# Order of the last scan group, spaced blocks for three weight tiles, and one changed row order in a hybrid decoder step

## The chip, the cores and the metric

The kernel is one launch on 1 core of one Trainium2 chip. The metric is the device time of a launch in microseconds (us). The version before was timed in 3 runs: median 1778.77 us, from 1777.38 to 1779.85.

## The reference, cut to what matters

One layer of a hybrid decoder is computed for 336 tokens (16 meta tokens, 256 prompt tokens, 8 sequences of 8 sample tokens), model width 2048, in float32:

```
h = rms_norm(x);  proj = h @ w_in          # z | x,B,C | dt | sc_b | sc_c | sc_h | sc_z | g_a | g_b
xbc = silu(causal_dwconv(x,B,C));  y, state = ssd_chunked(...)       # 64 heads in 8 groups
y   = gated_group_rms_norm(y + d_skip * xs, z);   y_a = y @ w_ssd_out
u   = sc_c * sc_h;  y_b = (sc_b * causal_dwconv(u) * silu(sc_z)) @ w_sconv_out
out = x + (sigmoid(g_a) * y_a + sigmoid(g_b) * y_b) @ w_o ;  final rms_norm
```

The gated norm divides each of the 8 groups (512 columns) of `y * silu(z)` by the root of its own mean square, so a group's output block `y @ w_ssd_out` needs that group's whole scan first.

## The kernel before, in words

**Products.** Every activation and every weight block is split into a high and a low part of the type that TensorE multiplies at full rate (`hi` by a copy on ScalarE, L101; `lo` by a subtraction on VectorE, L102), and each product is three matmuls: high by high, high by low, low by high. Weights come in blocks of 128x1024 through the SyncE queue (L98) into `wraw`, `whi` and `wlo`, three buffers each. A `unit` (two blocks, 48 matmuls, one PSUM buffer `pj` of two) gives 128 output columns for all tokens; the order of its 16 rows of weights is a plan: `SEVEN` starts at row 6 and steps by -2, `FIVE` likewise with another turn, a plain number starts at that row. In `whi` and `wlo` a 128-column block sits every 144 elements (`WS`, 576 bytes), and a start offset (`AT_O` and others, in 16 elements) is chosen for the activation that it meets. Three weight tiles are not stored so: `wd` (the 64 time-step columns, `tables`, L349 on) and `eh`, `el` (the last two output blocks, L833), whose blocks stand one behind the other, 512 bytes apart.

**Stages.** First the short convolution branch (pool `pa`): u's 16 columns are made by `conv_in`, the second of them (`j == 1`) straight from the unnormalised input split. Then `tables` makes the time steps and decays of all heads. Then the scan (pool `pb`), one group `g` of 8 at a time. Last, the output projection (pool `pc`): 14 blocks as units, the last two through `eh` and `el`, once with `hx` moving (L885) and once with `hx` as the weights (`tokens`, L911).

**One scan group.** `ssd(g)` is a generator with 24 stops. `weave` (L795 on) runs main units and lets the generator take its steps between them, `NSTEP` = 23 steps spread evenly over the units' weights (a unit of 48 matmuls weighs 2, an output block of 24 weighs 1). The main units of a group are `z_units` (4 units, the gate of the norm), `out_units(g-1)` (8 blocks that multiply the previous group's normalised output `yh`, `yl` and add into `ya`, L767), and `conv_units(g+1)` (6 units). Groups 0 and 7 have `gate_units` too (the g_a columns; each unit is a tanh on ScalarE and a store). In group 7 there are no conv units; before the change its order is z, out(6), gate 4 to 7. After the group come `out_units(7)` and `gate_units(8..15)`. Steps of the generator that matter here:

- step 13 sums the scan's output in PSUM and adds the parts to `ys`; steps 14 and 15 gate it with z and square it; step 16 adds the squares on GpSimd (L713) and loads the sample states' operands
- step 17 splits the sum of squares into `zq` (ScalarE L716, VectorE L717). `zq` has the one buffer of `yh`:

```
zq = pb.tile([P, 4, T], F32R, name="zq", tag="yh", bufs=1)[:, :, :TV]
...
yh = pb.tile([P, 4, T], F32R, name="yh", bufs=1)[:, :, :TV]
yl = pb.tile([P, 4, T], F32R, name="yl", bufs=1)[:, :, :TV]
```

- step 18 sums over the partitions with two matmuls (L721, PSUM buffer `ms`), takes a reciprocal root on ScalarE (L723, a function table of its own is loaded for it) and refines it twice on VectorE (six operations, L726 to L728)
- step 19 updates the prompt state (L608, `ms`) and the first half of the sample states (L736, `yb`; L739 on VectorE), step 21 scales `ys` and splits it into the new `yh`, `yl` (L749, L750, L751), step 22 is the second half of the sample states.

**What sets the order.** A tile framework plans each engine's queue ahead of the launch: it goes by the order of the program, lets an instruction pass another when the first must wait, and hands a buffer of a tag on only when every instruction that uses its last holder is done, wherever that instruction stands in the program. Matmuls into the same PSUM tag keep their order. `behind` adds that a step's instructions stand behind the last main unit's on each engine.

Of the kernel before, what the change touches and what calls it, by code (L numbers as in the profile page):

```python
# [8 lines left out]
F32R = mybir.dt.float32r  # L9
AF = mybir.ActivationFunctionType  # L10
# [3 lines left out]
P = 128  # L14
T = 336
WS, WB = 144, 1280
META = 16
TC = 12
TV = T - META
DM = 2048  # L20
KT = DM // P
NB = 8
NG = 8
NH = 64
# [3 lines left out]
NA, NBT = 192, 128  # L28
UE = 2
# [11 lines left out]
def fb(ap):  # L41
    return ap.bitcast(F32)
# [7 lines left out]
def tile_hybrid_step(ctx, tc, xT, w0, w1, w2, wdt, wso, wsc, wo, cmask, vec, hvec, convst, sconvst, xe_, fwe, h0T,  # L50
                     yA, yB, yE, convo, ssmp, ssms, sconvo):
    nc = tc.nc
    mult, add, sub = ALU.mult, ALU.add, ALU.subtract
# [19 lines left out]
    hx = keep.tile([P, 2, KT, T], F32R, name="hx")  # L73
    hhi, hlo = hx[:, 0], hx[:, 1]
# [16 lines left out]
    AT_V, AT_Y, AT_O, AT_X, AT_U = 1, 3, 3, 1, 2  # L91
# [20 lines left out]
                                                                         mybir.DependencyReason.DATA), reason="step")  # L112

    row = [0]
    SEVEN, FIVE, ON = (6, (7, 5, 5, 5), -2), (6, (5, 5, 5, 5), -2), (None, (5, 5, 5, 5), -2)

    def terms(plan, half, hi, lo, xh, xl, nk):
# [52 lines left out]
    def eights(ap, w=8):  # L170
        return ap.rearrange("p (b t) -> p b t", t=w)
# [17 lines left out]
    with tc.tile_pool(name="pa", bufs=2) as pa:  # L189
# [4 lines left out]
        raw = []  # L194
# [28 lines left out]
        for k in range(KT):  # L223
# [5 lines left out]
            if k % 2 == 0 or k == 1:  # L229
                o = slice(384 * k, 384 * k + 384) if k < 2 else slice(0, 768)  # L230
# [4 lines left out]
            for i, t0 in enumerate((TC, TC, META)):  # L235
                o = 384 * (k % 2) + i * P
                for j, (w, x) in enumerate(((hi, uhi), (hi, ulo), (lo, uhi))):
                    nc.tensor.matmul(pu[i][:, :T - t0], w[:, o:o + P], x[:, k, t0:],  # L238
                                     start=k == 0 and j == 0, stop=k == 15 and j == 2)
# [4 lines left out]
        def conv_in(j, pr, pre=None, fac=None, between=None, at=0):  # L244
            c_s = pa.tile([P, T - TC], F32, name="c_s")
            if fac is None:
                nc.scalar.activation(c_s, pre[0] if pre else pr(w2[16 + j], TC, SEVEN, at), AF.Copy)
            else:
                nc.vector.tensor_tensor(c_s, pr(w2[16 + j], TC, SEVEN, at), fac, mult)
            if between:  # L250
                between()
            ph = pre[1] if pre else pr(w2[32 + j], TC, ON, at)
            up = pa.tile([P, 338], F32, name=f"up{j}" if j < 2 else "up", bufs=1 if j < 2 else 2)
            ups = eights(up[:, 258:338], 10)
            nc.vector.tensor_tensor(up[:, :258], c_s[:, 2:260], ph[:, 2:260], mult)  # L255
            nc.vector.tensor_tensor(ups[:, :, 2:10], eights(c_s[:, 260:]), eights(ph[:, 260:]), mult)
            return up, ups
# [73 lines left out]
        for j in range(KT):  # L331
            u = ((up0, ups0), (up1, ups1), u2)[j] if j < 3 else conv_in(j, proj)
# [6 lines left out]
            if 4 < j < 7:  # L339
                o = j - 5  # L340
# [7 lines left out]
        def tables(pt):  # L348
            raw = wp.tile([P, 1024], F32, name="wraw")  # L349
            nc.sync.dma_start(raw, wdt)  # L350
            wd = pt.tile([P, KT, 2, NH], F32R, name="wd", bufs=1)
            nc.scalar.activation(wd[:, :, 0, :], eights(raw, NH), AF.Copy)
            nc.vector.tensor_tensor(wd[:, :, 1, :], eights(raw, NH), fb(wd[:, :, 0, :]), sub)
            pd = ps.tile([P, 512], F32, name="pj")
            for k in range(KT):
                w = wd[:, k].rearrange("p i h -> p (i h)")
                nc.tensor.matmul(pd[:, :T], w, hhi[:, k, :], start=k == 0, stop=False)
                nc.tensor.matmul(pd[:, :T], w, hlo[:, k, :], start=False, stop=k == KT - 1)
            yield
            xl = pt.tile([NH, T], F32, name="acc", bufs=1)  # L360
            nc.scalar.activation(xl, pd[NH:, :T], AF.Copy)
# [105 lines left out]
    with tc.tile_pool(name="pb", bufs=2) as pb:  # L467
# [51 lines left out]
        def z_units(g, st):  # L519
            st["zs"] = []  # L520
            for t in range(4):
                pz = proj(w1[4 * g + t], META, (0, 3, 3, 3, 1, 3, 2, 0)[g])
                z = pb.tile([P, TV + 4], F32, name="zs", bufs=4)
                th = pb.tile([P, 360], F32, name="cth", bufs=1)[:, :TV]
                nc.scalar.activation(th, pz, AF.Tanh, scale=0.5)
                nc.scalar.activation(z[:, :TV], pz, AF.Copy)
                nc.vector.scalar_tensor_tensor(z[:, :TV], th, 1.0, z[:, :TV], add, mult)
                st["zs"].append(z)
                yield
# [240 lines left out]
        def gate_units(m0, m1):  # L770
            for m in range(m0, m1):
                pg = proj(w2[64 + m], META, 2 if m in (6, 7) else 0)
                if m < KT // 2:
                    th = pb.tile([P, 360], F32, name="cacc")[:, :TV]
                else:
                    th = pb.tile([P, TV + 4], F32, name="zs", bufs=4)[:, :TV]
                nc.scalar.activation(th, pg, AF.Tanh, scale=0.5)
                if m < KT // 2:
                    nc.sync.dma_start(sg_d[m], th)
                else:  # L780
                    old = pb.tile([P, 360], F32, name="cacc")[:, :TV]
                    nc.sync.dma_start(old, sg_d[m - KT // 2])
                    pair = [(q, t, fetch(q)) for q, t in ((m, th), (m - KT // 2, old))]
                    with tc.issue_after(latest["dve"]):
                        for q in pair:
                            merge(*q)
                yield
# [25 lines left out]
            pass  # L813
        for g in range(NG):
            parts = [(z_units(g, S[g]), 4, 2)]
            if g:
                parts.append((out_units(g - 1, S[g - 1]), 8, 1))
            if g in (0, NG - 1):
                parts.append((gate_units(0, 4) if g == 0 else gate_units(4, 8), 4, 2))
            if g < NG - 1:  # L820
                parts.append((conv_units(g + 1, S[g + 1]), 6, 2))
            weave(parts, ssd(g, S[g]))
# [5 lines left out]
    with tc.tile_pool(name="pc", bufs=3) as pc_:  # L828
# [1 line left out]
            nc.scalar.activation(hhi[:, m, :TV], ya[:, m, :TV], AF.Copy)  # L830
            nc.vector.tensor_tensor(hlo[:, m, :TV], ya[:, m, :TV], fb(hhi[:, m, :TV]), sub)
        KE, W, PT = KT - UE, NA // 2, UE * P
        eh, el = (pc_.tile([P, UE, 2 * 1024], F32R, name=n, bufs=1) for n in ("eh", "el"))  # L833
        sacc = pc_.tile([P, TV], F32, name="sacc", bufs=1)
        fA = pc_.tile([P, KT, NA], F32, name="fA", bufs=1)
        fB = pc_.tile([P, KE, NBT], F32, name="fB", bufs=1)
# [34 lines left out]
        for m in range(KE, KT):  # L871
            xr = pc_.tile([P, TV], F32, name="xr")[:, :NA]
            nc.sync.dma_start(xr, xk[:, m, META:META + NA])
            po = ps.tile([P, 512], F32, name="pj")
            for half in range(2):
                o = 1024 * half
                raw = wp.tile([P, 1024], F32, name="wraw")
                nc.sync.dma_start(raw, wo[m][:, o:o + 1024])
                h, l = eh[:, m - KE, o:o + 1024], el[:, m - KE, o:o + 1024]
                nc.scalar.activation(h, raw, AF.Copy)  # L880
                nc.vector.tensor_tensor(l, raw, fb(h), sub)
                for wide in ((True, False), (False, True))[half]:
                    for k in range(8):
                        w, x = (h, hx[:, :, 8 * half + k, :NA]) if wide else (l, hhi[:, 8 * half + k, :NA])
                        nc.tensor.matmul(po[:, :(1 + wide) * NA], w[:, k * P:k * P + P], x,  # L885
                                         start=half + k == 0 and wide, stop=half == 1 and k == 7 and wide)
                if m == KT - 1 and half == 0:
                    with tc.issue_after(nc.cur_bb.bb.instructions[-1]):
                        p0 = ps.tile([P, 512], F32, name="ms")
                        for i in range(2):  # L890
                            column(p0, i, sacc, i * W, W)
                        column(p0, 2, sacc, NA, NBT)
                        for q, w in ((slice(0, 2), W), (slice(2, 3), P)):
                            nc.vector.tensor_scalar(sm[:w, q], p0[:w, q], 1.0 / DM, EPS, mult, add)
                        nc.vector.tensor_scalar(r[:, 3:4], p0[:, 2:3], 1.0, EPS * DM, mult, add)
                        nc.gpsimd.tensor_tensor(yt[:, PT:], r[:, 3:4], up_, ALU.pow)
            nc.vector.scalar_tensor_tensor(xr, po[:, :NA], 0.5, xr, mult, add)
            nc.vector.scalar_tensor_tensor(ya[:, m, :NA], po[:, NA:2 * NA], 0.5, xr, mult, add)
            s_ = pc_.tile([P, TV], F32, name="sqf")[:, :NA]
            nc.scalar.activation(s_, ya[:, m, :NA], AF.Square)  # L900
            if m < KT - 1:
                nc.gpsimd.tensor_tensor(sacc[:, :NA], sacc[:, :NA], s_, add)
            nc.scalar.activation(ya[:, m, :NA], ya[:, m, :NA], AF.Copy, scale=col(V_FW, m))
# [3 lines left out]
        def tokens(a, b):  # L907
            for k in range(a, b):
                x = hx[:, :, k, NA:TV]
                for j, (h, w) in enumerate(((0, eh), (1, eh), (0, el))):  # L910
                    nc.tensor.matmul(pt_, x[:, h, :], w[:, :, k * P:k * P + P], start=k == 0 and j == 0,  # L911
                                     stop=k == KT - 1 and j == 2)
            return nc.cur_bb.bb.instructions[-1]

# [144 lines left out]
```

## Time and profile before

| | |
|---|---|
| median of 3 runs | 1778.77 us |
| the profiled execution, whole | 1779.76 us |
| its span from first to last instruction | 1777.9 us |
| TensorE matmuls, busy | 13006, 1768.5 us |
| VectorE busy | 1145.9 us |
| ScalarE busy | 828.6 us |
| mean granted TensorE clock | 0.999 |

All rows are of one profiled execution. TensorE is busy in nearly all of the span, so a saving has to come from its matmuls following each other more closely or from its few waits; busy time of the other engines counts only where TensorE waits for them. A matmul's own duration is longer than the distance to the next one, since they overlap: what a matmul costs is the distance from start to start.

### The profile page before, as it was taken

What the parts mean: (1) busy time and instruction counts of PE and PEld (TensorE: products, weight loads), DVE (VectorE), ACT (ScalarE), POOL (GpSimd) and SP (SyncE); (2) the same over time, 40 slices, a digit from 0 to 9 for tenths busy, and PEclk for the clock granted to TensorE, in tenths of its full rate; (3) what the DMA queues carried; (4) which work ended last, traced back from release to release, by engine and by line L of the source; (5) the groups of instructions that cost most, each with busy time, mean ns of one, the idle gap of its engine ahead of it and who ended that gap; (6) DMA issues with size and microseconds to landing.
All of it is one profiled execution on the core that took longest, in us unless ns stands there. A gap on an engine that the chain in (4) does not pass through costs nothing.

```text
span 1777.9 us, 32410 instructions
## 1 busy us (share of the span) xinstructions
PE 1768.5 (99%) x13006; PEld 1751.2 (98%) x13006; DVE 1145.9 (64%) x1696; ACT 828.6 (47%) x1269; POOL 392.9 (22%) x398
## 2 busy tenths in 40 slices
PE   9999999999999999999999999999999999999998
PEld 9999999999999999999999999999999999999998
DVE  7845544544643335668587787877878778776644
ACT  6433333333333334645656454564546556343543
POOL 0100000000000001253253433434334252400012
PEclk9999999999999999999999999999999999999999
DMA  7444444444444557467466574665756657577553
GB/s 258 152 155 153 156 153 155 151 155 155 157 162 159 169 166 237 151 187 248 160 211 222 184 247 155 213 218 183 249 158 215 211 176 254 156 247 220 190 182 128
DMA packets 117286, 331.33 MB, mean 186 GB/s; under 512 B 20944, under 2 KB 37904, under 8 KB 117136
## 3 DMA queue, kind: packets, MB, share of 16 engines
q1 hardware_dynamic: 116272, 327.89, 56.9%
q8 instruction: 102, 1.67, 0.4%
q10 hardware_dynamic: 864, 1.38, 0.2%
q14 instruction: 48, 0.39, 0.1%
HBM read 296.34 MB, written 32.88 MB: 185 GB/s over the span
## 4 chain that ended last, share of the span: by engine, by line
PE 88%; DVE 5%; DMA 4%; ACT 2%; issue 1%; POOLq 0%; SPq 0%; POOL 0%; ACTq 0%; DVEq 0%
PE pj L133 81%; DMA wraw<-w 3%; PE yb L673 2%; DVE wlo L102 1%; DMA ssms<-h 1%; DVE h L739 1%; PE ms L659 1%; PE pj L238 1%; ACT whi L101 1%; DVE cacc L494 1%; ACT W L582 1%; PE yb L608 1%; PE pj L885 1%; PE ms L238 0%; PE yb L911 0%
## 5 line engine op out<-in xcount | busy, mean ns | idle before, releaser
L133 PE MATMUL pj<-hx,whi 128*128 128x320 f32 (+2 forms) x5760 | 894.7, 308 | 0.0
L133 PEld LDWEIGHTS pj<-hx,whi 128*128 128x128 f32 x5760 | 846.9, 188 | 4.7 <-ACT pad L485 1.7
L102 DVE TENSOR_TENSOR wlo<-wraw,whi 128x1024 fp32r<-128x1024 f32 x470 | 597.6, 1272 | 384.6 <-ACT whi L101 200.7
L101 ACT ACTIVATE whi<-wraw 128x1024 fp32r<-128x1024 f32 x470 | 496.5, 1057 | 719.3 <-PE pj L133 589.4
L133 PE MATMUL pj<-hx,wlo 128*128 128x320 f32 (+2 forms) x2880 | 473.5, 307 | 0.0
L133 PEld LDWEIGHTS pj<-hx,wlo 128*128 128x128 f32 x2880 | 430.7, 188 | 0.0
L619 POOL TENSOR_TENSOR h<-h,decS 128x512 f32<-128x512 f32 x64 | 76.4, 1227 | 141.8 <-PE ms L659 141.8
L133 PE MATMUL pj<-yh,whi 128*128 128x320 f32 x512 | 95.3, 308 | 2.6 <-DVE yan L767 1.4
L261 POOL COPY SCS<-up 128x2 f32<-128x2 f32 x16 | 20.9, 1303 | 346.1 <-DVE up L255 315.9
L133 PE MATMUL pj<-yl,whi 128*128 128x320 f32 x512 | 93.6, 305 | 0.0
L133 PE MATMUL pj<-yh,wlo 128*128 128x320 f32 x512 | 93.4, 304 | 0.0
L494 DVE SCALAR_TENSOR_TENSOR cacc<-pad,V,cacc 128x360 f32<-128x360 f32 (+1 forms) x144 | 89.7, 623 | 2.0
L767 DVE TENSOR_TENSOR yan<-yan,pj 128x320 f32<-128x320 f32 x112 | 53.8, 484 | 55.8 <-PE pj L133 55.5
L133 PEld LDWEIGHTS pj<-yh,whi 128*128 128x128 f32 x512 | 78.9, 188 | 5.9 <-DVE yan L767 2.2
L487 POOL COPY pad<-cs 128x24 f32<-128x24 f32 x48 | 56.2, 1172 | 126.4 <-DVE cacc L494 117.7
L133 PEld LDWEIGHTS pj<-yl,whi 128*128 128x128 f32 x512 | 78.7, 188 | 0.0
L133 PEld LDWEIGHTS pj<-yh,wlo 128*128 128x128 f32 x512 | 78.5, 188 | 0.0
L488 POOL COPY cs<-pad 128x3 f32<-128x3 f32 x48 | 45.4, 946 | 79.0 <-ACT pad L485 78.5
L867 POOL TENSOR_TENSOR sacc<-sacc,sqf 128x320 f32<-128x320 f32 x13 | 15.6, 1198 | 187.4 <-DMA wraw<-wo 120.5
L591 POOL TENSOR_TENSOR xe<-xdt,tet 128x512 f32<-128x512 f32 (+1 forms) x24 | 30.4, 1266 | 100.3 <-DVE xdt L562 100.3
L497 ACT ACTIVATE cth<-cacc 128x360 f32<-128x360 f32 (+1 forms) x48 | 24.0, 499 | 43.2 <-DVE cacc L494 42.9
L133 PE MATMUL pj<-vhi,wlo 128*128 128x320 f32 x256 | 41.5, 304 | 0.0
(284 smaller groups left out, 1634.6 us busy)
## 6 DMA issues: line engine op xcount, KB each, us to landing
wraw<-w SPq DMA_DIRECT2D x346, 512.0 KB, 3.8
wraw<-wso SPq DMA_DIRECT2D x64, 512.0 KB, 3.6
wraw<-wsc SPq DMA_DIRECT2D x32, 512.0 KB, 3.8
h<-h0T SPq DMA_DIRECT2D x32, 512.0 KB, 5.0
ssms<-h SPq DMA_DIRECT2D x32, 512.0 KB, 4.1
wraw<-wo SPq DMA_DIRECT2D x32, 512.0 KB, 3.9
xq_d<-xe SPq DMA_DIRECT2D x16, 320.0 KB, 3.3
W<-ac_d SPq DMA_DIRECT2D x8, 576.0 KB, 6.5
```

Of the source, the lines that this page charges most:

```text
L101: latest["act"] = nc.scalar.activation(hi, raw, AF.Copy).ins
L102: latest["dve"] = nc.vector.tensor_tensor(lo, raw, fb(hi), sub).ins
L133: latest["pe"] = nc.tensor.matmul(out, w[:, base + k], x(k0 + k), start=first and i == 0, stop=last and i == 3 * nk - 1).ins
L261: nc.gpsimd.tensor_copy(SCS[:, j, 0, :], up[:, 256:258])
L487: nc.gpsimd.tensor_copy(smp[:, :, 0:3], cs[:, 1:9, :])
L488: nc.gpsimd.tensor_copy(cs[:, 0, :], pad[:, 272:275])
L494: nc.vector.scalar_tensor_tensor(acc[:, i0:], pad[:, i0 + k:360 + k], col(V_CW, 4 * j + k), acc[:, i0:], mult, add)
L497: nc.scalar.activation(th[:, i0:], acc[:, i0:], AF.Tanh)
L591: nc.gpsimd.tensor_tensor(split(xe[c][:n]), split(xdt[c][:n]), bc(hv(tet[:n, c, :], g), [n, 8, HP]), mult)
L619: nc.gpsimd.tensor_tensor(split(h0[b]), split(h0[b]), bc(hv(decS[:, b, :], g), [P, 8, HP]), mult)
L673: nc.tensor.matmul(yb[q * HP:(q + 1) * HP, t, t0:t0 + n], x[:, h * HP:(h + 1) * HP], w[:, h, :], start=i == 0, stop=i == 3)
L767: nc.vector.tensor_tensor(ya[:, m, :TV], ya[:, m, :TV], pp[:, :TV], add)
```

## The change

Three edits. In group 7 the gate units 4 to 7 go between the z units and the output blocks of group 6, where they stood behind these. `wd`, `eh` and `el` get the layout of the other weights, blocks 576 bytes apart from an offset `AT_O`; the 32 matmuls of `wd` now run through all 16 rows with the high activation and then through all 16 with the low one. The second column of u (`j == 1`) takes a plan `FOUR` that starts at row 4 where `SEVEN` starts at row 6; the product after it goes on from there.

```
+    FOUR = (4, (7, 5, 5, 5), -2)
...
-                nc.scalar.activation(c_s, pre[0] if pre else pr(w2[16 + j], TC, SEVEN, at), AF.Copy)
+                nc.scalar.activation(c_s, pre[0] if pre else pr(w2[16 + j], TC, FOUR if j == 1 else SEVEN, at), AF.Copy)
...
-            wd = pt.tile([P, KT, 2, NH], F32R, name="wd", bufs=1)
-            nc.scalar.activation(wd[:, :, 0, :], eights(raw, NH), AF.Copy)
-            nc.vector.tensor_tensor(wd[:, :, 1, :], eights(raw, NH), fb(wd[:, :, 0, :]), sub)
+            wd = pt.tile([P, WB + KT * WS - 8 * WS], F32R, name="wd", bufs=1)[:, 16 * AT_O:16 * AT_O + KT * WS].rearrange("p (k m) -> p k m", m=WS)
+            nc.scalar.activation(wd[:, :, :NH], eights(raw, NH), AF.Copy)
+            nc.vector.tensor_tensor(wd[:, :, NH:P], eights(raw, NH), fb(wd[:, :, :NH]), sub)
             pd = ps.tile([P, 512], F32, name="pj")
-            for k in range(KT):
-                w = wd[:, k].rearrange("p i h -> p (i h)")
-                nc.tensor.matmul(pd[:, :T], w, hhi[:, k, :], start=k == 0, stop=False)
-                nc.tensor.matmul(pd[:, :T], w, hlo[:, k, :], start=False, stop=k == KT - 1)
+            for i in range(2):
+                for k in range(KT):
+                    nc.tensor.matmul(pd[:, :T], wd[:, k, :P], hx[:, i, k, :], start=i + k == 0, stop=i == 1 and k == KT - 1)
...
             parts = [(z_units(g, S[g]), 4, 2)]
+            if g in (0, NG - 1):
+                parts.append((gate_units(0, 4) if g == 0 else gate_units(4, 8), 4, 2))
             if g:
                 parts.append((out_units(g - 1, S[g - 1]), 8, 1))
-            if g in (0, NG - 1):
-                parts.append((gate_units(0, 4) if g == 0 else gate_units(4, 8), 4, 2))
...
-        eh, el = (pc_.tile([P, UE, 2 * 1024], F32R, name=n, bufs=1) for n in ("eh", "el"))
+        eh, el = (pc_.tile([P, 16 * AT_O + UE * KT * WS], F32R, name=n, bufs=1)[:, 16 * AT_O:].rearrange("p (u k m) -> p u k m", u=UE, m=WS)[..., :P] for n in ("eh", "el"))
...
-                h, l = eh[:, m - KE, o:o + 1024], el[:, m - KE, o:o + 1024]
-                nc.scalar.activation(h, raw, AF.Copy)
-                nc.vector.tensor_tensor(l, raw, fb(h), sub)
+                h, l = (e[:, m - KE, 8 * half:8 * half + 8] for e in (eh, el))
+                nc.scalar.activation(h, eights(raw, P), AF.Copy)
+                nc.vector.tensor_tensor(l, eights(raw, P), fb(h), sub)
...
-                        nc.tensor.matmul(po[:, :(1 + wide) * NA], w[:, k * P:k * P + P], x,
+                        nc.tensor.matmul(po[:, :(1 + wide) * NA], w[:, k], x,
...
-                    nc.tensor.matmul(pt_, x[:, h, :], w[:, :, k * P:k * P + P], start=k == 0 and j == 0,
+                    nc.tensor.matmul(pt_, x[:, h, :], w[:, :, k], start=k == 0 and j == 0,
```

## The prediction

> **What bounds the kernel now.** I read the page first, then the stretches of group 7 by engine, then the order of time around its two ends, then single lines.
>
> ```profile
> PE 1768.5 (99%) x13006; PEld 1751.2 (98%) x13006; DVE 1145.9 (64%) x1696; ACT 828.6 (47%) x1269; POOL 392.9 (22%) x398
> ```
>
> TensorE (PE) is busy for 99% of the span. The whole execution took 1779.76 us, 0.99 above the median of the three runs; I make the sum against it and take the 0.99 off at the end. So there is little to win: a wait of TensorE taken away, or matmuls that follow each other faster. There is much more to lose, because anything that opens a new wait shows at its full length.
>
> ```profile
> core 0: us, PE busy (x) PEld busy (x) DVE busy (x) ACT busy (x) POOL busy (x), PEclk, DMA share, GB/s
> 1510.30:1546.20 35.90, 34.69 (x328) 33.54 (x327) 27.74 (x44) 13.86 (x23) 15.76 (x13) 1.00 0.45 138
> 1546.20:1575.50 29.30, 29.30 (x207) 28.36 (x205) 21.55 (x31) 16.25 (x23) 6.04 (x4) 1.00 0.76 251
> 1771.60:1775.10 3.50, 0.71 (x4) 0.52 (x4) 1.62 (x3) 0.79 (x2) 1.55 (x2) 1.00 0.76 281
> 1775.10:1777.90 2.80, 0.00 (x0) 0.00 (x0) 0.00 (x0) 0.00 (x0) 0.00 (x0) 0.51 0.54 209
> ```
>
> The first two rows are the parts of group 7 that change places: output blocks of group 6, then gate units 4 to 7. In the second TensorE never rests. In the first it lacks 1.2 us; the lines in order of time say where:
>
> ```profile
> 1511.64 0.73 PE L133 MATMUL pj<-yh,wlo 128*128 128x320 f32 x4
> 1513.58 0.86 PE L133 MATMUL pj<-yh,whi 128*128 128x320 f32 x4 [1.22 <-ACT zs L526]
> ```
>
> The group's last z unit leaves its PSUM buffer to ScalarE, which empties it late (L526), and the second half of the first output block, only 12 matmuls later, needs that buffer. The second wait of the group is at its end:
>
> ```profile
> 1578.46 0.73 PE L133 MATMUL pj<-yh,wlo 128*128 128x320 f32 x4
> 1579.57 0.71 PE L133 MATMUL pj<-yh,whi 128*128 128x320 f32 x3 [0.38 <-DVE yan L767]
> ```
>
> **The change, part by part.** *The old waits.* Four matmuls that start at 1511.64 and last until 1512.37 start some 0.14 apart, so the fifth was due at 1512.20 and came at 1513.58: 1.4 us lost. With a gate unit behind the z units the next PSUM buffer is needed 48 matmuls later, some 6.8 us, against a lateness of 1.4. In the same way the fifth after 1578.46 was due at 1579.03 and came at 1579.57: 0.5 us lost, because VectorE was late with its adds. Both should go, the second because VectorE gets idle time ahead of out(7) (next point). Minus 1.9; bounds 0 and minus 1.9.
>
> *The new wait.* This is the step that decides. The generator's steps stay where they are in TensorE's work, since the weights of the units are the same: 7 steps beside the z units, 8 beside the next 8 weights, 8 beside the last. But in place of the gate units the last 8 weights are now the output blocks of group 6, and these read `yh` until their last matmul. Step 17 falls behind the second of the eight blocks, and its tile `zq` sits in the one buffer of `yh`. So `zq` cannot be written before the last output block is through; that block in turn must not stand behind the norm's sum in TensorE's queue, or nothing could go on, and since the two use different PSUM tags the planner can let the blocks pass. Behind the last block TensorE then needs the new `yh` for out(7), and everything that makes it has only then begun. Before, the same chain was spread over 29 us of gate units:
>
> ```profile
> 1545.98 0.74 PE L133 MATMUL pj<-yh,wlo 128*128 128x320 f32 x4
> ...
> 1560.20 0.45 PE L721 MATMUL ms<-zq,CR 128*128 128x320 f32 x2
> ...
> 1575.52 0.84 PE L133 MATMUL pj<-yh,whi 128*128 128x320 f32 x4
> ```
>
> ```profile
> 1552.42 0.47 ACT L716 ACTIVATE zq<-zs 128x320 fp32r<-128x320 f32 x1 [4.32 <-POOL zs L713]
> ...
> 1561.77 1.28 ACT L723 ACT_TABLE_LOAD   x1
> 1563.07 0.53 ACT L723 ACTIVATE ms_r<-ms,eps 128x320 f32<-128x320 f32 x1
> ...
> 1573.41 0.87 ACT L750 ACTIVATE yh<-ys 128x320 fp32r<-128x320 f32 x2
> ```
>
> ```profile
> 1567.40 0.48 DVE L727 TENSOR_TENSOR ms_a<-ms_a,ms_r 128x320 f32<-128x320 f32 x1
> 1567.91 0.49 DVE L728 SCALAR_TENSOR_TENSOR ms_r<-ms_a,ms_r 128x320 f32<-128x320 f32 x1
> ...
> 1571.04 1.47 DVE L749 SCALAR_TENSOR_TENSOR ys<-ys,V,ms_r 128x320 f32<-128x320 f32 x3
> ```
>
> The last reads of the old `yh` end at 1546.7, and `zq` began 5.7 us later, released by GpSimd's L713: in the kernel before, the shared buffer cost nothing. Its cover was the order. Now the chain counts from the last matmul of out(6): the copy 0.47, the table load 1.28, the root 0.53, six VectorE operations 0.51 apart (1567.40 to 1567.91), 3.1, and from the first L749 to the end of the last L750, 1571.04 to 1574.28, 3.2: together 8.6 us. The subtraction to `zq`, about as long as L727, and the two matmuls, 0.45, lie beside the table load. Three matmuls of out(7) can go early, 0.4; and the two of the norm's sum drop out of TensorE's path into the gap, 0.4. Net plus 7.8. Bounds: 7.0, if VectorE makes the four scalings in one go (0.49 each, 2.0, and one copy of 0.47, in place of 3.2); 11, if the table load waits for the sum (1.0 more) and VectorE puts a weight split (1.27) and an add to the sample states (1.21, both rows below) into the chain. I take 7.8, because these rows show the links as VectorE really mixes them.
>
> *The clock.* TensorE would rest for over 8 us with little in between. No rest of that length is in this trace, but its two ends bound it:
>
> ```profile
> 1.24 4.63 PE L207 MATMUL ms<-warm 128*128 128x128 f32 x20 [1.24 <-DVE warm L192]
> ...
> 6.46 0.59 PE L238 MATMUL pj<-uhi,wlo 128*128 128x324 f32 x1
> ...
> 7.24 0.31 PE L238 MATMUL pj<-uhi,wlo 128*128 128x324 f32 x1
> ```
>
> At the start the same matmul takes 0.59 and, after 5.8 us of work, 0.31. At the end the granted clock is 0.51 from 1775.10 on, in a stretch behind 3.5 us with 0.71 of matmuls. So a rest of 8 us should halve the clock, and after it TensorE runs at half speed for somewhere between 0 and 5.8 us, which costs 0 to 2.9. I take 2.0, nearer to the upper row, since out(7) starts from as cold a state. The Trainium skill, page "TensorE: Matmul & The Clock Gate", Part 1 and the table of "Why this matters for your kernels", gives a window of about 3.4 us, halves the clock after one idle window and restores it after one busy window, and so warns against gaps over 3 us: this speaks against the change, and by it the price would be an estimated 1.7 to 3.4 (one to two windows at half speed). The end of this trace agrees (0.51).
>
> *The spaced blocks.* Nothing is added: the same 32, 64 and 48 matmuls, and copies and subtractions of the same sizes. What they could win:
>
> ```profile
> 466.08 2.45 PE L133 MATMUL pj<-hx,whi 128*128 128x320 f32 x16
> 468.38 1.30 PE L133 MATMUL pj<-hx,wlo 128*128 128x320 f32 x8
> ...
> 1756.30 2.99 PE L885 MATMUL pj<-hx,eh 128*128 128x384 f32 x16
> 1759.12 1.03 PE L885 MATMUL pj<-hx,el 128*128 128x192 f32 x8
> ```
>
> Spaced blocks run 16 matmuls of 320 columns from 466.08 to 468.38, 0.144 each or 0.45 ns a column, hence 0.173 for 384; `eh` takes 2.82 / 16 = 0.176. So some 3 ns each, over the 144 matmuls of the three tiles 0.4: I take minus 0.4, bounds 0 and minus 0.6. The tile `wd` is larger by 1536 bytes and moves the tiles behind it; that is a whole number of 512-byte steps, and I expect nothing of it, bounds plus and minus 0.5. The Trainium skill, same page, Part 2, step 1, says that loading the next weights does not take read bandwidth from the running matmul; by that rule the spacing is worth nothing and the sum is 0.4 higher.
>
> *`FOUR`* touches 96 matmuls of two products; at most a few ns on the first of a block: 0, bounds plus and minus 0.3.
>
> Sum: minus 1.9, plus 7.8, plus 2.0, minus 0.4 gives plus 7.5. The profiled execution would be 1787.3 and the median 1786.3 us.
>
> **The rivals.** *The copy does not wait.* If the norm's sum got a place of its own, or in some way ran ahead of the last reads of `yh`, the order would be what it seems: two waits fewer. Then VectorE decides, since steps 16 to 23 now stand beside output blocks.
>
> ```profile
> L102 DVE TENSOR_TENSOR wlo<-wraw,whi 128x1024 fp32r<-128x1024 f32 x470 | 597.6, 1272 | 384.6 <-ACT whi L101 200.7 <-PE pj L133 178.8 <-PE ms L560 2.9
> ...
> L767 DVE TENSOR_TENSOR yan<-yan,pj 128x320 f32<-128x320 f32 x112 | 53.8, 484 | 55.8 <-PE pj L133 55.5
> ...
> L739 DVE TENSOR_TENSOR h<-h,yb 128x1024 f32<-128x1024 f32 x32 | 38.7, 1212 | 0.0
> ```
>
> Eight blocks cost it 8 x (1.27 + 2 x 0.48) = 17.9, the steps 4 x 1.21 + about 16 operations of 0.49 = 12.7, together 30.6 in a stretch of 29.3: late by 1.3, which it can hide behind three buffers of weights. That gives minus 2.3 to minus 1.0 by the same terms, a median of 1776.5 to 1777.8: not slower. It decides if L716 starts before the last matmul that reads the old `yh`. For it: the rows show L716 waiting for L713 alone; against it: the tag in the code.
>
> *The clock stays up.* Then only the chain counts: 1784.3. For it: the sum's matmuls and the sample states' may fall into the gap and keep TensorE awake; against it, the 0.71 us of matmuls in 3.5 did not keep the clock at the end.
>
> *A longer chain.* VectorE and ScalarE work for out(7) is queued between the links, and the table load waits: 3 us more, 1789.3.
>
> *The gap is filled.* The planner could draw the gate units 8 to 15 ahead of out(7). It decides if a weight buffer and a `pj` are free for them; but out(7) comes first in the program and takes both. It would give about 1776.5.
>
> **How the numbers follow.** My forecast at 1786.3 gets 0.50, the clock that stays up 0.20, the longer chain 0.15, the copy that does not wait 0.10, the filled gap 0.05. A measurement of this kernel can tell 0.2%, 3.6 us, from no change, so slower means above 1782.3 and faster below 1775.2. The first three are slower: 0.85. Of the others nearly all lies within 0.2%: same 0.13, faster 0.02. The range leaves out the rivals at 1776 to 1778 and the outer ends of the bounds: from 1782.5 (chain 7.0, clock 0, spaced blocks minus 0.6, and minus 0.8 for the moved tiles and `FOUR`) to 1791.0 (chain 11, clock 2.9, spaced blocks 0).
>
> **What would show it.** Right: L716 of group 7 starts just behind the last matmul of out(6) with a wait put down to TensorE; TensorE idles once for 6 to 10 us ahead of the first out(7) matmul, put down to L749 or L750; a granted clock near 0.5 in the slices around it; the waits at L526 and L767 gone; L885 and L911 a few ns shorter. Wrong: L716 early and no such gap, or a gap with gate matmuls in it.

## The result, and the profile after

The changed kernel takes 1790.28 us (median of 5 runs, 1789.57 to 1790.67) against 1778.77 before: a ratio of 1.0065, 95% interval 1.0053 to 1.0076, or 11.5 us more by the medians. The forecast was 1786.3, with a range up to 1791.0. The span of the profiled execution grew from 1777.9 to 1788.5 us. (Below, one execution of `e7`, 6329.6 us and the one that was profiled, and one of `e11`, 6874.7 us, lie far outside all others of their kernels and are left out of the ratios.) The page's line of engine totals first, then TensorE's waits around group 7 (engine, line, what it waited for: us in total, times, longest):

```profile
PE 1772.2 (99%) x13006; PEld 1753.8 (98%) x13006; DVE 1146.8 (64%) x1696; ACT 829.7 (46%) x1269; POOL 389.5 (22%) x398
```

```profile
PE pj L134 <- ACT yh L750: 5.9, 2, 5.4
PE ms L721 <- ACT zq L716: 0.9, 1, 0.9
PE ms L721 <- DVE zq L717: 0.8, 1, 0.8
PE pj L134 <- ACT whi L101: 0.5, 1, 0.5
PE pj L134 <- ACT cacc L777: 0.3, 1, 0.3
PE pj L134 <- DVE yan L767: 0.3, 1, 0.3
```

The instructions are the same in number and the engines are busy for almost as long as before; what changed is mainly their order. The two old waits, on L526 and behind out(6) on L767, are gone. In their place stand the three links of the chain to the new `yh` (first three rows), 7.6 us, and three short waits inside out(6), 1.1 us. The stretch between out(6) and out(7) in order of time (start, length, engine, line, operation, written and read, and in brackets the idle time before it and who ended it; rows that the argument does not need are left out):

```profile
1573.94 0.73 PE L134 MATMUL pj<-yh,wlo 128*128 128x320 f32 x4
1574.14 1.06 ACT L101 ACTIVATE whi<-wraw 128x1024 fp32r<-128x1024 f32 x1 [3.00 <-PE pj L134]
1575.10 0.45 ACT L716 ACTIVATE zq<-zs 128x320 fp32r<-128x320 f32 x1
1575.37 1.22 DVE L102 TENSOR_TENSOR wlo<-wraw,whi 128x1024 fp32r<-128x1024 f32 x1
1575.57 1.28 ACT L723 ACT_TABLE_LOAD   x1
1576.50 0.48 DVE L717 TENSOR_TENSOR zq<-zs,zq 128x320 fp32r<-128x320 f32 x1
1577.04 0.41 PE L721 MATMUL ms<-zq,CR 128*128 128x320 f32 x1 [0.79 <-DVE zq L717]
1577.49 0.53 ACT L723 ACTIVATE ms_r<-ms,eps 128x320 f32<-128x320 f32 x1 [0.64 <-PE ms L721]
1578.05 0.49 DVE L724 TENSOR_SCALAR ms_x<-ms 128x320 f32<-128x320 f32 x1 [0.47 <-ACT ms_r L723]
...
1582.37 1.33 ACT L750 ACTIVATE yh<-ys 128x320 fp32r<-128x320 f32 x3 [4.35 <-DVE ys L749]
1582.89 2.11 PE L134 MATMUL pj<-yh,whi 128*128 128x320 f32 x6 [5.44 <-ACT yh L750]
1585.42 0.63 PE L134 MATMUL pj<-yh,whi 128*128 128x320 f32 x1 [0.42 <-ACT yh L750]
1585.86 1.27 PE L134 MATMUL pj<-yl,whi 128*128 128x320 f32 x4
...
1590.23 0.75 PE L134 MATMUL pj<-yh,whi 128*128 128x320 f32 x4
```

`zq` starts 0.4 us behind the end of the last matmul of out(6) (1574.67); in the kernel before it started 23 us ahead of out(7). At 1585.86 four matmuls take 1.27 us, at 1590.23 four take 0.75. The stretches show the clock (us, busy time and count of each engine, then PEclk, the granted clock):

```profile
1574.70:1579.70 5.00, 1.05 (x3) 0.48 (x3) 4.43 (x9) 2.66 (x4) 0.00 (x0) 1.00 0.98 292
1579.80:1589.90 10.10, 6.58 (x23) 6.07 (x24) 5.91 (x13) 2.14 (x5) 0.00 (x0) 0.50 0.25 96
```

### The profile page after: what moved, and what is told of

The parts are those of the page before. It is cut to its first block, busy times and chain, and to the rows that moved or that the text cites. A ratio compares the mean times of both kernels' runs of the same rounds, so it can differ in the third digit from the quotient of the medians.

```text
span 1788.5 us, 32410 instructions
## 1 busy us (share of the span) xinstructions
PE 1772.2 (99%) x13006; PEld 1753.8 (98%) x13006; DVE 1146.8 (64%) x1696; ACT 829.7 (46%) x1269; POOL 389.5 (22%) x398
## 4 chain that ended last, share of the span: by engine, by line
PE 94%; DVE 3%; ACT 1%; DMA 1%; issue 1%; POOLq 0%; POOL 0%; ACTq 0%; SPq 0%; DVEq 0%
PE pj L134 87%; PE yb L673 2%; DMA wraw<-w 1%; PE ms L659 1%; PE pj L239 1%; DVE wlo L102 1%; PE yb L608 1%; ACT whi L101 1%; PE pj L885 1%; PE ms L557 0%; PE ms L239 0%; DVE h L739 0%; PE yb L911 0%; PE yb L736 0%; ACT W L582 0%
## 5 line engine op out<-in xcount | busy, mean ns | idle before, releaser
L102 DVE TENSOR_TENSOR wlo<-wraw,whi 128x1024 fp32r<-128x1024 f32 x470 | 596.8, 1270 | 391.9 <-ACT whi L101 208.5
L767 DVE TENSOR_TENSOR yan<-yan,pj 128x320 f32<-128x320 f32 x112 | 53.9, 485 | 60.0 <-PE pj L134 59.6
L134 PE MATMUL pj<-vlo,whi 128*128 128x320 f32 x256 | 41.5, 305 | 0.0
```

What stands on the lines that cost most here:

```text
L102: latest["dve"] = nc.vector.tensor_tensor(lo, raw, fb(hi), sub).ins
L134: latest["pe"] = nc.tensor.matmul(out, w[:, base + k], x(k0 + k), start=first and i == 0, stop=last and i == 3 * nk - 1).ins
L767: nc.vector.tensor_tensor(ya[:, m, :TV], ya[:, m, :TV], pp[:, :TV], add)
```

## The experiments

The theory: `zq` sits in the buffer of `yh`, so the whole norm stands in series between out(6) and out(7), and the rest costs the clock. The rivals: the other edits (moved tiles, spaced blocks); VectorE overloaded beside the output blocks; the order as such.

**The two halves of the change.** The kernel before with the order alone (`e4`), and the changed kernel with the old order (`e3`):

```
# e4, from before
 parts = [(z_units(g, S[g]), 4, 2)]
+if g in (0, NG - 1): parts.append((gate_units(...), 4, 2))    # moved up from below
 if g: parts.append((out_units(g - 1, S[g - 1]), 8, 1))
# e3, from after: the same two parts put back
```

> The kernel before with the new order of group 7 alone: no spaced blocks, no FOUR. The theory (zq waits in the buffer of yh for out(6), the serial chain and the clock behind it) puts the whole loss into the order: 1790.5 us, with TensorE idle once for some 8 us ahead of out(7) and the granted clock at half behind it. If the layout of wd, eh and el or their moved tiles had a part in the loss, this kernel would stand clearly under 1790: 1778 if they were all of it.

> The changed kernel with the old order of group 7 (z, out, gate); the spaced blocks and FOUR stay. Theory 1: the time of before less what the spacing and FOUR give, 0.2 for wd and 0.1 for FOUR by the starts in the two traces: 1778.5 us, which a measurement cannot tell from before. Theory 3: 1788 or more.

`e4`: 1791.43 us, ratio 1.0066 (1.0052 to 1.0079). `e3`: 1777.42 us, ratio 0.9997 (0.9988 to 1.0006). The order alone gives the whole loss; what the spaced blocks and `FOUR` do together cannot be told from nothing (the interval of `e3` goes from 2.1 us less to 1.1 more).

**The shared buffer.** `zq` in another tag (`e1`); in `e2` the new `yh` and `yl` of group 7 get places of their own too:

```
-zq = pb.tile([P, 4, T], F32R, name="zq", tag="yh", bufs=1)[:, :, :TV]
+zq = pb.tile([P, 2, 576], F32R, name="zq", tag="E", bufs=1)[:, :, :TV]
# e2 also: yh in tag "xs0", yl in tag "xs1" when g == NG - 1
```

> The changed kernel with one line different: the split sum of squares zq takes the buffer of the tag E, which is free by then, and not that of yh; the new yh and yl still follow the old ones in their own buffers. Theory 1 (buffer): the norm's sum, root and refinement run beside the last output blocks; behind out(6) only the copies to the new yh and yl are left, four by 0.47 on ScalarE, so TensorE waits 1.4 to 2 us and not 8.4, and the clock stays up; 1790.3 - 6.7 - 3.5 = 1780 us. Theory 2 (VectorE beside the output blocks is too slow): VectorE gets more to do beside the blocks than in the changed kernel, so the time does not fall, about 1788 to 1790. Theory 3 (the spaced blocks and their larger tiles cost the time): nothing changes, 1790.

> As e1, and in group 7 the new yh and yl also take buffers that are free by then (xs0 and xs1), so that no step of the norm waits for out(6). Theory 1: no wait ahead of out(7) is left but what VectorE makes; 1790.3 - 8.4 - 3.5 = 1778.4 us, plus 0 to 2 for VectorE, whose 30.6 us of work now all lie beside 28 us of output blocks. Theory 2: 1788 to 1790. Theory 3: 1790.

`e1`: 1782.81 us, ratio 1.0021 (1.0011 to 1.003). `e2`: 1782.74, ratio 1.0022 (1.0013 to 1.0031). One tag gives back some 7.5 of the 11.5 us, and in both profiled executions the clock stays at full: that half of the theory stands. But both expected less time than came. TensorE's waits of `e2`, and in order of time what released the longest:

```profile
PE pj L134 <- DVE yan L767: 3.8, 3, 2.0
...
```

```profile
1542.36 4.58 POOL L713 TENSOR_TENSOR zs<-zs 128x320 f32<-128x320 f32 x3 [0.93 <-ACT zs L697]
1542.51 3.72 DVE L102 TENSOR_TENSOR wlo<-wraw,whi 128x1024 fp32r<-128x1024 f32 x2
1546.97 0.47 ACT L716 ACTIVATE zq<-zs 128x320 fp32r<-128x320 f32 x1 [2.62 <-POOL zs L713]
1547.47 0.49 DVE L717 TENSOR_TENSOR zq<-zs,zq 128x320 fp32r<-128x320 f32 x1 [1.25 <-ACT zq L716]
1547.88 0.88 DVE L767 TENSOR_TENSOR yan<-yan,pj 128x320 f32<-128x320 f32 x2
1548.42 0.86 PE L134 MATMUL pj<-yh,whi 128*128 128x320 f32 x4 [1.99 <-DVE yan L767]
...
1562.79 1.21 DVE L739 TENSOR_TENSOR h<-h,yb 128x1024 f32<-128x1024 f32 x1
...
1564.32 0.88 DVE L767 TENSOR_TENSOR yan<-yan,pj 128x320 f32<-128x320 f32 x2
...
1564.95 0.83 PE L134 MATMUL pj<-yh,whi 128*128 128x320 f32 x4 [1.42 <-DVE yan L767]
```

The row behind these waits is the 0.3 on L777 that the changed kernel has too. GpSimd's additions hold ScalarE, ScalarE holds VectorE for 1.25 us at the subtraction to `zq`, and behind that subtraction stand the adds (L767) that give the output blocks their PSUM buffers back. An output block wants a buffer every 1.7 us, a gate unit every 6.8, and a gate unit's buffer is emptied by ScalarE. In the second long wait VectorE does not stand still: two L739 and other work are queued ahead of the adds. From start to start the four waits cost 0.47, 2.15, 1.58 and 0.56 us, together 4.8, which is 2.9 more than the two old ones. That fits the profiled execution, the shortest of its ten: 1780.59 us, 2.3 over the 1778.3 of the kernel before in the same session. By the ratio `e2` loses 3.9 us (2.3 to 5.5). The clock may be the rest: the mean granted clock is 0.999 in the profiled execution, but 0.998 in seven of the ten, against one of 27 of the kernel before. The trace of `e11` (next) shows a drop that lowers the mean by as much; no trace of `e2` does.

**Too much work on VectorE, or what stands ahead in its queue?** Both from `e2`, in group 7 alone: `e10` drops two of the three GpSimd additions, `e11` the four L739:

```
-for t in range(1, 4):
+for t in range(1, 4 if g < NG - 1 else 2):     # e10, ahead of L713
...
+if g < NG - 1:                                 # e11, around L739
```

> The order of the change with every buffer of its own (second kernel of the first set: 1782.74 us, waits of 0.47, 2.15, 1.58 and 0.56 inside and behind out(6)); in group 7 two of the three GpSimd additions of the squares (L713) are left out, so the norm of that group is not the reference's. The theory (VectorE's queue stands still because its subtraction to zq waits for ScalarE's copy, which waits for GpSimd, and the adds that free the output blocks' PSUM stand behind it): the wait of 2.15 us goes to 0.5 or less, the wait of 1.58 stays: 1780.5 to 1781.5 us. The rival (VectorE has simply too much work there, 30.6 us in 29.3): the wait only moves, since no VectorE work is taken away: 1782.5.

> The same kernel with every buffer of its own; in group 7 the four adds to the sample states on VectorE (L739, 1.21 us each) are left out, so those states are not the reference's. The theory: the wait of 1.58 us, ahead of which two of these adds stand in VectorE's queue, goes; the wait of 2.15, which has another cause, stays: 1781 us. The rival (too much work on VectorE as a whole): with 4.8 us of work less all four waits go, and the time is 1778.5.

`e10`: 1781.33 us, ratio 1.0015 (1.0005 to 1.0024). `e11`: 1781.67, ratio 1.0016 (1.0006 to 1.0026). In the times each is only 1.1 to 1.4 us under `e2`, and the intervals overlap. The waits tell them apart, first of `e10`, then of `e11` (its lines from L740 on are one higher):

```profile
PE pj L134 <- DVE yan L767: 1.9, 2, 1.4
...
```

```profile
PE pj L134 <- DVE yan L768: 2.0, 1, 2.0
...
```

In both the 0.3 on L777 stays. `e10` took no work from VectorE and lost the 2.0; `e11` took 4.8 us of work from it and kept the 2.0, losing only the other two. So it is not a total of work but what stands ahead of the adds in a queue that is served in order: the first time a subtraction that must wait, the second time a burst of work. The first has a smaller part beside the 1.25 us: the two weight splits (L102) ahead of the subtraction took 3.72 us beside GpSimd's three additions, 3.05 beside the one of `e10`, and 2.37 in `e8` with GpSimd idle. The Trainium skill, page "TensorE: Matmul & The Clock Gate", Part 1, says that VectorE and ScalarE are strictly first in, first out; these runs agree.

`e11` missed the 1781 by little, but its profiled execution (1780.52 us) also paid for its wait of 2.0 us in another way: the granted clock halved behind it for 3.4 us (below), and 14 matmuls took 3.7 us where 2.0 is the full pace. The same wait in the trace of `e2` left the clock at 1.00.

```profile
1546.00:1549.41 3.41, 1.40 (x10) 1.15 (x10) 2.15 (x5) 1.42 (x2) 1.65 (x1) 1.00 0.90 262
1549.42:1552.82 3.40, 3.40 (x14) 3.40 (x14) 1.49 (x3) 0.00 (x0) 0.00 (x0) 0.50 0.96 308
```

**The price of the clock.** 64 dummy matmuls of 128 columns, into a PSUM tile that nobody reads, between group 7 and out(7):

```
+fill = ps.tile([P, 512], F32, name="pj")
+for _ in range(64):
+    nc.tensor.matmul(fill[:, :P], onesR, hx[:, 0, 0, :P], start=True, stop=True)
```

> The changed kernel with 64 extra matmuls of 128 columns, whose result nobody reads, traced between out(6) and out(7): they lie in the gap, 64 x 0.11 = 7.0 us of its 8.4. Theory 1 with the clock as its second part: the granted clock stays at 1.0 through the gap and out(7) starts at full pace, 3.5 us less: 1786.8 us. If the slow start of out(7) is not the clock but its late operands: 1790 still, or a little more. The chain of the norm itself is not touched, so the first out(7) matmul comes as late as in the changed kernel.

1788.82 us, ratio 1.0058 (1.0044 to 1.0072). The clock stays up in the stretches, but the last part of `yh` still ends the wait:

```profile
1577.50:1584.00 6.50, 6.50 (x58) 6.50 (x59) 5.79 (x13) 1.83 (x4) 0.00 (x0) 1.00 0.69 222
1584.00:1590.00 6.00, 4.75 (x32) 4.49 (x32) 3.07 (x7) 1.56 (x3) 0.00 (x0) 1.00 0.00 0
```

```profile
1585.75 0.42 PE L134 MATMUL pj<-yh,whi 128*128 128x320 f32 x1 [1.25 <-ACT yh L750]
```

So keeping TensorE busy won some 1.5 us (the intervals of the two ratios overlap), not the 3.5 expected. In the changed kernel's trace 3.0 of the 7.1 us from the first matmul of out(7) at half clock (1582.89 to 1585.86) lay under the wait for `yh` and cost nothing. And in `e5` only four matmuls of out(7) went ahead of its first yl, not seven, because the dummies ran until 1584.0: that costs `e5` 0.4 us.

**How much cover is needed?** One, two or three of the four gate units ahead of out(6), the rest behind it (`e6`, `e8`, `e7`):

```
+if g == NG - 1: parts.append((gate_units(4, 4 + n), n, 2))       # n = 1, 2, 3
 if g: parts.append((out_units(g - 1, S[g - 1]), 8, 1))
+if g == NG - 1: parts.append((gate_units(4 + n, 8), 4 - n, 2))
```

> The changed kernel with one gate unit, not four, between z units and output blocks; three stand behind them. The theory: the one unit is enough to take away the wait of 1.4 us behind the z units, the last read of yh comes before the step that makes zq, so there is no chain and no gap, and the norm's steps stand beside gate units again: 1776.5 to 1777.5 us. Rival (any output block behind a gate unit is late on VectorE, whatever stands beside it): waits of 0.5 to 2 us inside out(6) stay, 1778 to 1781.

> The changed kernel with two gate units ahead of out(6) and two behind it. zq falls beside the middle of the output blocks and must wait for their end, some 7 us; the chain of 10.9 us then starts with two gate units (13.6 us) still to run ahead of out(7), so the theory gives no gap and no slow clock: 1777 to 1779 us. If a wait of zq by itself were harmful, whatever stands behind it, the time would be nearer to 1785.

> The changed kernel with three gate units ahead of out(6) and one behind it: a dose between. The chain of 10.9 us runs beside one gate unit of 6.8 us, so some 3 to 4 us of idle TensorE are left ahead of out(7), with at most a short drop of the clock; beside it waits of about 1 us within out(6), since more of the norm's steps stand beside output blocks. The theory: 1781 to 1783 us. A loss that hangs on the order as such and not on the length of cover would give about 1787 to 1790.

`e6`: 1778.11 us, ratio 0.9992 (0.9983 to 1.0001). `e8`: 1777.37, ratio 0.9987 (0.9978 to 0.9996), 2.3 us under the kernel before: the fastest order by its ratio, though by less than the 0.2% that was set as the bound, and the intervals of `e3` and `e6` overlap with it. `e7`: 1787.5, ratio 1.004 (1.0025 to 1.0056).

In `e8` the only wait left around group 7 is 0.2 us, although `zq` waits for out(6) as the theory says it must:

```profile
PE ms L721 <- ACT zq L716: 0.2, 1, 0.2
```

```profile
1556.61 0.73 PE L134 MATMUL pj<-yh,wlo 128*128 128x320 f32 x4
...
1557.77 0.45 ACT L716 ACTIVATE zq<-zs 128x320 fp32r<-128x320 f32 x1
...
1569.08 1.54 ACT L750 ACTIVATE yh<-ys 128x320 fp32r<-128x320 f32 x4
...
1572.98 0.84 PE L134 MATMUL pj<-yh,whi 128*128 128x320 f32 x4
```

The copy comes 0.4 us behind the end of the last matmul of out(6) (1557.34), as in the changed kernel, and `yh` is done 2.4 us before out(7) needs it. The same wait for the same buffer costs no more than that 0.2 with two gate units behind it.

`e7` missed its expectation by 4.5 us and left no usable trace, so it was run once more:

> Three gate units first, once more, since the profiled run before was one of 6329.6 us in which every matmul took about three times as long, so it shows no usable times; the others were at 1785 to 1788. In its order of instructions the last refinement of the root stands on VectorE behind the adds to the sample states (L739), which wait for matmuls (L736) that TensorE does at the end of the gate unit. The theory now: the gate unit covers only the first half of the chain, and what comes behind the unit (two adds of 1.21, L728, L749, L750: some 4 to 5 us) is idle ahead of out(7); 1785 to 1788 us. If the chain were covered as first expected, the wait ahead of out(7) would be 3 to 4 us less the part that ran early and the time 1781 to 1783.

1787.32 us, ratio 1.0046 (1.0031 to 1.0061). The end of its gate unit in order of time, then the clock:

```profile
1571.84 0.49 DVE L726 SCALAR_TENSOR_TENSOR ms_a<-ms_r,ms_x 128x320 f32<-128x320 f32 x1
...
1573.05 1.23 DVE L102 TENSOR_TENSOR wlo<-wraw,whi 128x1024 fp32r<-128x1024 f32 x1 [0.72 <-PE pj L134]
1574.19 0.48 DVE L727 TENSOR_TENSOR ms_a<-ms_a,ms_r 128x320 f32<-128x320 f32 x1
1574.60 1.22 DVE L739 TENSOR_TENSOR h<-h,yb 128x1024 f32<-128x1024 f32 x1
1575.73 0.48 DVE L728 SCALAR_TENSOR_TENSOR ms_r<-ms_a,ms_r 128x320 f32<-128x320 f32 x1
...
1578.42 2.11 PE L134 MATMUL pj<-yh,whi 128*128 128x320 f32 x6 [5.03 <-ACT yh L750]
```

```profile
1573.60:1578.40 4.80, 0.00 (x0) 0.00 (x0) 4.80 (x8) 1.56 (x4) 0.00 (x0) 0.92 0.55 212
1578.40:1584.20 5.80, 5.35 (x18) 4.84 (x19) 2.93 (x7) 1.31 (x3) 0.00 (x0) 0.50 0.70 247
1584.40:1590.00 5.60, 5.60 (x41) 5.60 (x40) 3.23 (x5) 2.12 (x2) 0.00 (x0) 1.00 0.30 95
```

VectorE stops between L726 and L727: its next instruction is a weight split that must wait for the gate unit's last matmuls to give up a buffer. The norm's last half is queued behind it, so this gate unit is no cover for it. VectorE is then busy for the whole idle stretch of TensorE.

## Why the prediction was right, and where its sizes were off

- *The old waits, minus 1.9.* Right: both are gone.
- *The new wait, plus 7.8.* The mechanism is right: `e1` undoes it with one tag. The size was too small, and this is the largest miss of the sum, 2.2 us. In a run without waits the fifth matmul after 1573.94 is due at 1574.51 and the eighth of out(7) (the first yl) seven distances of 0.142 later, 1575.50; it came at 1585.86. That is 10.4, less 0.4 for the two matmuls of the sum: 10.0. The chain measured 10.9 (1574.51 to 1585.42) where 8.6 was summed: 0.6 until `zq` starts, behind a weight copy on ScalarE; 0.6 because a weight split stands ahead of L717 on VectorE, so the end of the sum came behind the table load and not beside it; 0.5 because L724 waited for the root (0.47 in its row) and was not counted as a link; 0.5 in L749 and L750. Seven matmuls went early, not three. The prediction had put the weight split into its upper bound of 11 (its parts give 11.3, and the range's end of 1791.0 goes by that) and taken a value near the lower one: links measured while the engines had slack were summed for a stretch in which they have none.
- *The clock, plus 2.0.* The drop is right: the 17 matmuls from 1585.86 to 1590.23 took 4.4 us, 2.4 at the full pace. That the size is right too is in part luck: out(7) ran at half clock for 7.1 us, where at most 5.8 were allowed for, and only the wait for the last of `yh` hid 3.0 of them, which the prediction did not foresee. The rival of a clock that stays up is refuted by the stretch at 0.50.
- *Waits inside out(6).* This is the term that the prediction left out. It gave them a place only in its first rival, "late by 1.3, which it can hide behind three buffers of weights". In the changed kernel they are 1.1 us by the waits, 1.6 by distances from start to start; with `zq` elsewhere they are 4.1 and 4.8 (`e2`). Three weight buffers do not help, since in `e2` each of the three longest waits is for VectorE to hand back one of the two PSUM buffers (in the changed kernel one of three, 0.5, is for a weight copy). So the rival's 1776.5 to 1777.8 was wrong by some 5 us: a copy that does not wait brings the norm's steps forward into out(6), and the order is still slower than before.
- *The spaced blocks, minus 0.4.* Half of that. `wd` runs faster, by the line of its 32 matmuls and the next one after and the first one before:

```profile
460.78 4.92 PE L358 MATMUL pj<-hx,wd 128*128 128x336 f32 x32
465.54 0.75 PE L134 MATMUL pj<-hx,whi 128*128 128x320 f32 x4
```

```profile
461.14 0.32 PE L357 MATMUL pj<-hx,wd 128*128 128x336 f32 x1
```

  32 distances take 4.76 us after, and 4.94 before (461.14 to 466.08 in the prediction's row): 0.18 less, of which the new order of the rows may have a part, as neither run splits the two. `eh` and `el` keep their distances:

```profile
1766.85 2.98 PE L885 MATMUL pj<-hx,eh 128*128 128x384 f32 x16
1769.66 1.03 PE L885 MATMUL pj<-hx,el 128*128 128x192 f32 x8
```

  That is 2.81 for 16, against 2.82; the 48 matmuls of L911 take 6.94 us from first start to last, against 6.92, so these did not get shorter either. The rule of the Trainium skill that the prediction weighed (page "TensorE: Matmul & The Clock Gate", Part 2, step 1) agrees with these two tiles; only `wd` may speak against it, and there the row order changed too. `FOUR` and the moved tiles: nothing that `e3` can show.
- *The rivals.* The gap filled by gate units and the copy that does not wait are refuted: no gate matmul stands in the gap, and `zq` starts behind the last matmul of out(6). The longer chain, at 1789.3 with a chance of 0.15, is what came nearest: weight work for out(7) does stand between the links, as it says, though the table load did not wait.

The sum of the measured terms: minus 1.9, plus 10.0, plus 2.0, plus 1.6, minus 0.2 is 11.5. The medians agree with it, but the terms come from two single traces, and the spans of these differ by 10.6. Of the 0.9 between, 0.5 lies ahead of the change: the first matmul behind the z units of group 7 starts 0.7 us earlier after (1509.69 against 1510.39), of which `wd` gives 0.2 and no term the rest. The other 0.4 stays open. The total of the prediction, plus 7.5, is 4 us short of this; it stayed within its range because that range took in a longer chain, not because the waits were foreseen.

## What to carry to other kernels

Before work is moved, look up what each step of the other stream reads and which buffer it writes: the work that leaves may have been the cover of a shared buffer, and `e8` shows that such a wait is free where the whole chain fits beside the work behind it. Cover counts only for links that are not queued behind the covering work itself: in `e9` one gate unit of 6.8 us hid the first half of the chain and nothing of the second, because VectorE's next instruction needed that unit's last matmuls. And sum a chain for the place to which it moves, with the weight copies and splits that the engines must do there, not with the gaps it had where it was measured.

## What the runs showed of the hardware

The granted clock changes in equal steps of time of about 3.4 us: it is at 0.50 for three steps in the changed kernel (1579.8 to 1590.0), for two in `e9` (1577.6 to 1584.4) and for one in `e11` (1549.4 to 1552.8). TensorE's busy time in the step ahead of each drop was 0.4, 0.0 and 1.4 us. In `e2` the wait of 2.0 us falls across an edge, counted in steps of 3.41 from the drop at the end of its trace (1776.02): the steps on both sides, from 1543.9 and from 1547.3, have 2.2 and 2.3 us of matmuls, and the clock stayed. So a wait of 2 us can halve the clock or not, by where it falls; 1.4 us of work in a step were too little here and 2.2 were enough.

The clock came back 7.1 us after TensorE started again in the changed kernel and 6.0 in `e9` (1578.42 to 1584.4), both with a break of 0.4 us in between, each time at the end of the first step that TensorE worked through without a break. The Trainium skill, page "TensorE: Matmul & The Clock Gate", Part 1, states a free-running window of 3413 ns and a full clock after one busy window; this agrees if the window with the break (3.0 us of matmuls in the changed kernel) did not count as busy, which no run here tests by itself. The other half of the rule that the prediction quotes, a drop after one idle window, is too narrow for `e11`, whose window was not idle; there the trace decides. Had TensorE had all its data from 1582.89 on, 7.1 us at half pace would have cost 3.5, more than the prediction's upper bound of 2.9; as it was, part of the slow time lay under the wait.

In the changed kernel L724 only reads the PSUM tile that L723 reads as well, and yet it started 0.03 us after L723's end, put down to it (0.47 idle). Whether the chip or the planned order asks for that stays open.
